# Two six-tile groups of the down projection by seven half-size products, with smaller edits in the delta rule and at both ends of the span

## The chip, the core and the metric

The kernel runs on one core of a Trainium2 chip. The metric is the device time in microseconds of one execution, from launch to the last store. A profile of one execution is at hand as well; its span is the time from the first to the last instruction on the core's engines.

## What is computed

One decoder layer on 1024 tokens of width 1024, in float32 (the leading depth axis has length 1):

```python
def hybrid_layer(x, p_i, ...):
    h = rmsnorm(x, g_mix)
    proj = h @ w_in
    ...
    y_fox = forgetting_attention(fq, fk, fv, fox_f, b_fox_f, fox_q_gain, fox_k_gain)
    ...
    y_sc = sb * causal_dwconv(sc * sv, sc_conv_w)
    ...
    o_dn = gated_delta_rule(l2norm(dq), l2norm(dk_), dv_, g, beta).astype(x.dtype)
    ...
    merged = jnp.sum(jnp.einsum('bsnc,ncd->bsnd', ys, w_branch) * gates, axis=2)
    x = x + merged @ w_o
    u = causal_dwconv(rmsnorm(x, g_ffn) @ w_up, ffn_conv_w)
    u_gate, u_val = jnp.split(u, 2, axis=-1)
    x = x + (jax.nn.silu(u_gate) * u_val) @ w_down
    x = x + jax.nn.sigmoid(rmsnorm(x, g_ple) @ w_ple_gate) * (p_i.astype(x.dtype) @ w_ple)
    return x
```

The inner width of the channel mixer is 2816, that is 22 tiles of 128; `w_down` is 2816 by 1024.

## The kernel before

Activations lie transposed, 128 channels on the partitions and 1024 tokens along the free axis, so a tile is 128 by 1024 and has two halves of 512 tokens (`NB`). Each float32 operand of a large product is split into a high part (rounded to the TensorE's fp32r) and a low part: `split` (lines 128 to 130) copies the high part on ScalarE and subtracts it on VectorE (or GpSimd). `step` (151) then makes three matmuls of 128 by 512: high by high, high by low, low by high. `dense` (159) does this for every k tile and hands the two PSUM banks to an evacuation function. Weights come in by `wraw` into a tile `wr` (two buffers of 1024 columns) and are split by `wsplit` into `wo` (five buffers, high in columns 0 to 511 and low in 512 to 1023).

The program goes: first norm and input projection with attention (`first_norm`, `fox_proj`, `softmax`, `weigh`), the delta rule (`dn_solve`, `dn_prep`, `dn_state`, `dn_out`), with projection tiles used as filler work between, the merge and `W_o`, the up projection, the down projection ("do"), and a last stage that normalises the result, multiplies it by `w_ple_gate` and adds the gated per-layer embedding.

The code is written in program order, and a scheduler at build time sets the order in which each engine's queue gets its instructions. At run time each queue is strictly in order: an instruction that waits holds up what stands behind it on its engine. This is so for SyncE's queue too, which issues nearly all DMAs.

In the up projection, 20 of 22 tiles are made with Strassen's scheme (Winograd's form): `stationary` makes four sums of quarter blocks of the weights and gives seven stationaries, `moving_sums` does the same for the activations, and `seven` (203) runs seven products per pair of output tiles where plain blocking takes eight. It uses three PSUM banks a, b, c per pair: product 1 into a (copied out by ScalarE as s1), 6 added into a (copied out as u2), 7 into b, 5 added into a (copied out as v), then, among the next pair's products, 3 added into a and 4 added into b. The outputs are c + s1, a, b + u2 and b + v. A product that is added into a bank must wait for the copy that was taken from it. There are six banks `mm` and two `sm` in this part.

Down is plain. The 22 activation tiles are taken in `GROUPS` of 2, 4, 4, 4, 4, 4. Tiles 2 and 3 were kept in SBUF; the others come back from DRAM into `wq` (three buffers) and are split by `act`. For each group and each of the four pairs of output tiles (`d2`), one `wload` brings 256 columns of weights per activation tile, `dense` multiplies, and VectorE adds the PSUM bank into `x2` (lines 1172 to 1182), which began as the residual.

The last stage (1184 to 1201): for each of the eight `x2` tiles, `sumsq` squares on ScalarE and adds the squares on GpSimd into two accumulators, and `norm_operand` makes the operands for the gate product. `make_rstd` (283) splits each accumulator, sums over partitions with two matmuls per half into a bank `sm`, and makes the reciprocal root with Ln, Exp and Square on ScalarE and two operations on VectorE. The gate products do not need that factor, but their evacuation does: `ev_f` multiplies the bank by `rs3`, takes the sigmoid, multiplies by the embedding, adds `x2` and stores.

Lines of the delta rule that the change touches: in `add64` (759), two groups of four 128 by 128 float32 matmuls, into `px` and `pt_`, and a VectorE subtraction of the whole `pt_`; in `dn_prep` (803 to 807), the sums of squares of q by four float32 matmuls with one moving column. Line 1271 in the profile is the program's prologue.

## Time and profile before

| | |
|---|---|
| median of three runs | 1966.72 us (1966.46 to 1970.54) |
| profiled execution | 1967.07 us, of which the span is 1965.1 us |
| TensorE matmul busy | 98% of the span |
| VectorE, ScalarE, GpSimd busy | 68%, 46%, 27% |
| DMA, mean over the span | 112 GB/s |
| up projection, down, last stage | from about 1200, 1635 and 1875 us |

The page has the busy time of each engine, the chain of work that ended last, and groups of instructions with the mean of one and the idle time before them. Other views give windows (the busy time of each engine in a stretch of time), waits (who waited for whom), and a timeline (instructions in order of time: start in us from the span's start, duration or the extent of a merged group, engine, line, operation, and in brackets the idle time before it and what ended it). In every view, the mean of one matmul is from its issue until its modelled end, so it is longer than the distance between two that follow each other. A float32 matmul appears as two entries.

### The profile page before, as it was taken

How to read it: one execution, taken by the hardware profiler on the slowest of the kernel's cores; microseconds unless marked ns; L12 is line 12 of the kernel's file. 1: busy time of each engine (PE TensorE's matmuls, PEld its weight loads, DVE VectorE, ACT ScalarE, POOL GpSimd, SP SyncE). 2: the span in 40 equal slices, each digit the busy share in tenths (PEclk: the TensorE clock that was granted, in tenths of full speed). 3: DMA queues.
4: the chain of work that ended last, by engine and by line, in shares of the span. 5: the costliest groups of instructions: out<-in, count | busy, mean ns of one | idle time of the engine just before them, and what ended most of it. 6: DMA issues, size and time to landing. Idle time of an engine off the chain costs nothing.

```text
span 1965.1 us, 25454 instructions
## 1 busy us (share of the span) xinstructions
PE 1930.3 (98%) x9281; PEld 1605.9 (82%) x9281; DVE 1331.0 (68%) x2161; ACT 910.8 (46%) x1651; POOL 531.9 (27%) x431
## 2 busy tenths in 40 slices
PE   8999999999999999999999999999999999999998
PEld 6888888888888888888788787788888887888887
DVE  6878788879388213437766538888888888444564
ACT  6576777677422223433433326555445453211351
POOL 1446343434412221100034112244333330000200
PEclk9999999999999999999999999999999999999999
DMA  4221112221432144347863523212212218322132
GB/s 179 71 91 68 58 60 73 68 69 58 134 127 102 51 148 124 113 175 265 282 223 117 188 107 110 73 61 79 97 64 97 80 49 289 97 86 86 44 119 85
DMA packets 102636, 219.40 MB, mean 112 GB/s; under 512 B 9360, under 2 KB 40432, under 8 KB 102512
## 3 DMA queue, kind: packets, MB, share of 16 engines
q1 hardware_dynamic: 102512, 217.79, 32.8%
q8 instruction: 73, 1.20, 0.3%
q14 instruction: 51, 0.42, 0.1%
HBM read 158.98 MB, written 58.77 MB: 111 GB/s over the span
## 4 chain that ended last, share of the span: by engine, by line
PE 75%; DVE 11%; DMA 5%; ACT 4%; issue 3%; POOL 1%; SPq 0%; DVEq 0%; ACTq 0%; POOLq 0%
PE mm L126 65%; PE sm L126 5%; DVE o L491 1%; DMA sg<-r 1%; PE py L126 1%; PE ev L126 1%; PE pq L637 1%; DVE wo L130 1%; DMA kc<-kdr 1%; DMA y<-yr 1%; DVE o L1094 1%; PE po L126 1%; DMA yr<-r 1%; DVE pl L130 1%; ACT pp L600 1%
## 5 line engine op out<-in xcount | busy, mean ns | idle before, releaser
L126 PE MATMUL mm<-xg,wo 128*128 128x512 f32 x6128 | 1478.9, 392 | 9.4 <-DVE wo L130 2.1
L126 PEld LDWEIGHTS mm<-xg,wo 128*128 128x128 f32 x6128 | 1139.2, 188 | 247.5 <-ACT wo L129 3.5
L126 PE MATMUL mm<-a,wo 128*128 128x512 f32 x1216 | 303.5, 389 | 1.6 <-DVE sg L1029 1.4
L129 ACT ACTIVATE wo<-wr 128x512 fp32r<-128x512 f32 x252 | 157.2, 626 | 278.0 <-PE mm L126 269.9
L126 PEld LDWEIGHTS mm<-a,wo 128*128 128x128 f32 x1216 | 228.2, 188 | 49.8 <-DVE sg L1029 1.8
L130 POOL TENSOR_TENSOR wo<-wr,wo 128x512 fp32r<-128x512 f32 x108 | 150.2, 1393 | 312.4 <-ACT wo L129 299.0
L1181 DVE TENSOR_TENSOR a<-mm,a 128x512 f32<-128x512 f32 x96 | 65.2, 688 | 92.2 <-PE mm L126 92.0
L130 DVE TENSOR_TENSOR wo<-wr,wo 128x512 fp32r<-128x512 f32 x144 | 106.6, 742 | 27.9 <-ACT wo L129 27.4
L280 POOL TENSOR_TENSOR tmp<-tmp,tmp 128x512 f32<-128x512 f32 x21 | 28.1, 1339 | 293.3 <-ACT tmp L278 293.3
L1030 POOL TENSOR_TENSOR a<-a,sg 128x512 f32<-128x512 f32 x28 | 42.4, 1521 | 190.9 <-DVE sg L1029 190.8
L1094 DVE SCALAR_TENSOR_TENSOR o<-cw,cols,o 128x1024 f32<-128x1024 f32 x44 | 77.2, 1755 | 0.0
L491 DVE SCALAR_TENSOR_TENSOR o<-cv,cols,o 128x512 f32<-128x512 f32 x72 | 69.9, 971 | 10.1 <-ACT o L489 9.1
L503 ACT ACTIVATE o<-mm 128x512 f32<-128x512 f32 x60 | 35.7, 595 | 88.3 <-PE mm L126 52.1
L1126 POOL TENSOR_TENSOR cg<-o,cg 128x1024 f32<-128x1024 f32 x22 | 54.8, 2492 | 62.8 <-ACT cg L1125 62.8
L600 ACT ACTIVATE pp<-pp,small 128x512 f32<-128x512 f32 (+2 forms) x96 | 58.4, 610 | 28.9 <-DVE small L594 28.6
L130 DVE TENSOR_TENSOR wo<-wq,wo 128x512 fp32r<-128x512 f32 x48 | 65.4, 1365 | 5.0 <-ACT wo L129 4.2
L129 ACT ACTIVATE wo<-ws 128x512 fp32r<-128x512 f32 x80 | 50.2, 630 | 33.4 <-PE mm L126 33.3
L199 POOL TENSOR_TENSOR ws<-wq,wr 128x512 f32<-128x512 f32 x20 | 44.0, 2199 | 78.9 <-DVE wo L130 73.9
L1094 DVE SCALAR_TENSOR_TENSOR o<-cg,cols,o 128x1024 f32<-128x1024 f32 x44 | 58.4, 1327 | 5.0 <-ACT o L1092 4.9
L130 DVE TENSOR_TENSOR pl<-pq,ph 128x512 fp32r<-128x512 f32 (+1 forms) x80 | 49.9, 629 | 13.9 <-ACT ph L129 13.5
L199 POOL TENSOR_TENSOR ws<-wr 128x512 f32<-128x512 f32 x20 | 35.9, 1797 | 72.3 <-DVE ws L199 46.3
L637 PE MATMUL pq<-cst,pp 128*128 128x128 f32 x288 | 47.0, 273 | 2.0 <-DVE pl L130 1.1
(291 smaller groups left out, 2362.3 us busy)
## 6 DMA issues: line engine op xcount, KB each, us to landing
wr<-win SPq DMA_DIRECT2D x64, 512.0 KB, 3.6
r<-o SPq DMA_DIRECT2D x64, 256.0 KB, 2.5
wq<-wup SPq DMA_DIRECT2D x24, 512.0 KB, 3.5
wr<-wup SPq DMA_DIRECT2D x20, 512.0 KB, 3.7
ad<-o SPq DMA_DIRECT2D x20, 512.0 KB, 3.9
wq<-ad SPq DMA_DIRECT2D x20, 512.0 KB, 4.6
wr<-wdn SPq DMA_DIRECT2D x20, 512.0 KB, 3.7
yr<-r SPq DMA_DIRECT2D x16, 512.0 KB, 5.0
```

The source lines that it names most:

```text
L126: pe[0] = nc.tensor.matmul(o, lhsT=l, rhs=r, start=start, stop=stop, skip_group_check=more)
L129: S.activation(h, x, AF.Copy)
L130: (eng or V).tensor_tensor(out=l, in0=x, in1=h.bitcast(F32), op=ALU.subtract)
L199: (G if e == "g" else V).tensor_tensor(out=o, in0=x, in1=y, op=op)
L491: V.scalar_tensor_tensor(out=o, in0=cv[:, i : i + 512], scalar=col(c0 + i), in1=o, op0=ALU.mult, op1=ALU.add)
L503: S.activation(o, ps, AF.Copy)
L600: S.activation(t[:, :w], t[:, :w], AF.Exp, bias=mn[:, k - 1 : k], scale=-1.0, accum_out=sm[:, i : i + 1])
L637: nc.tensor.transpose(pq[:, c : c + P], pr[s][kt // 4][:, kt % 4 * P : kt % 4 * P + P], ident)
L1030: (V if b == 2 and dt > 5 else G).tensor_tensor(out=m, in0=m, in1=t, op=ALU.add)
L1094: V.scalar_tensor_tensor(out=o, in0=cv[:, i : i + T], scalar=col(c0 + i), in1=o, op0=ALU.mult, op1=ALU.add)
L1126: G.tensor_tensor(out=sg, in0=o, in1=sg, op=ALU.mult)
L1181: V.tensor_tensor(out=x2[dt][:, NB[nb]], in0=ps, in1=x2[dt][:, NB[nb]], op=ALU.add)
```

## The change

1. The groups of down are now of 2, 4, 6, 4 and 6 tiles. A group of six goes to the new function `down`: three pairs of activation tiles are the two halves of k, `moving_sums` makes their sums on VectorE, 21 operand tiles are made (seven in new `bx` buffers, eight in `a`, six in `xg`), and `seven` runs over the four pairs of output tiles, with weights of 768 columns for each half of k, both in `wr`.
2. `seven` now hands every finished bank to a function `ev`. In up it does what was done before. In down, a bank without partner is added into `x2` by VectorE, one with a partner is added to it by VectorE, and the sum goes to `x2` on GpSimd or VectorE.
3. `add64` makes only the 64 by 64 part of `pt_` that is used later. `dn_prep` splits the squares of q and sums them with two fp32r matmuls of two columns per head.
4. At the start, the loads of `cols` and `wsr` are issued by ScalarE's queue, and the first activation tile is loaded in two halves. At the end, the last output half-tile is made and stored in two pieces of 256 columns.
5. The last stage has a scope of its own ("ple"), so its temporaries take the memory of the down stage's when that is done with.

```diff
-GROUPS = [KEPT, (0, 1, 4, 5), (6, 7, 8, 9), (10, 11, 12, 13), (14, 15, 16, 17), (18, 19, 20, 21)]
+GROUPS = [KEPT, (0, 1, 4, 5), (6, 8, 10, 7, 9, 11), (12, 13, 14, 15), (16, 18, 20, 17, 19, 21)]
...
-    Q.dma_start(cols, I["cols"])
+    S.dma_start(cols, I["cols"])
...
-                S.activation(o12, oa, AF.Copy)
+                oev(0, 1, oa)
...
-                V.tensor_tensor(out=c11, in0=c, in1=s1, op=ALU.add)
+                ev(0, 0, c, s1)
...
-        Q.dma_start(wsr, I["wsm"])
+        S.dma_start(wsr, I["wsm"])
...
-            Q.dma_start(xr[kt], I["xT"][kt])
+            for nb in NB if kt == 0 else (slice(0, T),):
+                Q.dma_start(xr[kt][:, nb], I["xT"][kt][:, nb])
...
-                mm(pt_[:, hs(h)], ws[c][:, hs(h)], Tc[c][:, h, :], True, True)
+                mm(pt_[0:64, h * 64 : h * 64 + 64], ws[c][0:64, h * P : h * P + 64], Tc[c][0:64, h, 0:64], True, True)
...
+        qh, ql = pt("qh", 2, 512, F32R), pt("ql", 2, 512, F32R)
         S.activation(qe, qc, AF.Square)
+        split(qh, ql, qe)
         pq_ = evb()
         for h in range(4):
-            mm(pq_[:, h : h + 1], qe[:, hs(h)], Uf[:, 127:128], True, True)
+            mm(pq_[:, 2 * h : 2 * h + 2], qh[:, hs(h)], ones_r[:, 0:2], True, False)
+            mm(pq_[:, 2 * h : 2 * h + 2], ql[:, hs(h)], ones_r[:, 0:2], False, True)
...
-        with phase("do", tmp=8, sg=4):
+        x2 = [ahead[dt] for dt in range(8)]
+        with phase("do", u=4, ws=3):
...
+            def down(f, c0):
+                xs = {k: [] for k in range(1, 8)}
+                room = [xgt] * 6 + [lambda: big(F32R)] * 8 + [lambda: pt("bx", 7, T, F32R)] * 7
...
+                for i in range(3):
+                    b1, b2 = (fetch(k) and acts[k] for k in (f[i], f[i + 3]))
+                    for k, x in ((1, b1[:, NB[0]]), (2, b2[:, NB[0]]), (3, b2[:, NB[1]])):
+                        xs[k].append(operand(x, new))
+                    for k, t in moving_sums(b1, b2, new, "vvvv").items():
+                        xs[k].append(t)
+                def pair(d2):
+                    w = [wraw(I["wdn"][:, c : c + 768], 768) for c in range(c0 + 1536 * d2, c0 + 1536 * d2 + 1536, 768)]
+                    def ev(m, nb, ps, more=None):
+                        o = x2[2 * d2 + m][:, NB[nb]]
+                        V.tensor_tensor(out=o if more is None else more, in0=ps, in1=o if more is None else more, op=ALU.add)
+                        if more is not None:
+                            (G if m == nb else V).tensor_tensor(out=o, in0=o, in1=more, op=ALU.add)
+                    return stationary(*w, 384), ev, lambda: None
+                seven([lambda d2=d2: pair(d2) for d2 in range(4)], xs)
...
+        with phase("ple", tmp=8, sg=4):
             acc = [tmp() for _ in range(2)]
...
+                    gs, n = tmp(), 256 if (dt, nb) == (7, 1) else 512
+                    for c in range(0, 512, n):
```

On TensorE, this is what stands around the sums of squares of the last norm (`sm` is the bank of a sum, `tmp` a part of the squares, `mm` the bank of a gate product). Before:

```order
L126 MATMUL mm_16079<-xg_15991,wo_16043 128x512
L126 MATMUL mm_16079<-xg_16003,wo_16043 128x512
L126 MATMUL mm_16079<-xg_16004,wo_16043 128x512 [waits DVE_49]
L126 MATMUL sm_16028<-tmp_16015,ones_r 128x512 [waits DVE_49]
L126 MATMUL mm_16079<-xg_16003,wo_16043 128x512
L126 MATMUL mm_16120<-xg_15919,wo_16114 128x512
L126 MATMUL mm_16120<-xg_15920,wo_16114 128x512
```

And now:

```order
L126 MATMUL sm_16335<-tmp_16328,ones_r 128x512 [waits DVE_49]
L126 MATMUL mm_16544<-xg_16320,wo_16508 128x512
L126 MATMUL sm_16345<-tmp_16331,ones_r 128x512 [waits Activation_49]
L126 MATMUL sm_16345<-tmp_16332,ones_r 128x512 [waits DVE_49]
L126 MATMUL mm_16585<-xg_16236,wo_16579 128x512 [waits DVE_49]
L126 MATMUL mm_16585<-xg_16237,wo_16579 128x512
```

Before, the sums stood among the first two gate products (banks 16046 and 16079), and the third began behind them without a wait. Now six gate products (16363, 16396, 16437, 16470, 16511, 16544) stand ahead of the sums, and the seventh, 16585, begins with a wait for VectorE: the instruction that its semaphore value belongs to is the evacuation of bank 16363.

On VectorE, behind the same sums (L260 and L264 are the last two operations of each half of the norm factor `rs`, L1196 and L1240 the first of an evacuation). Before:

```order
L260 SCALAR_TENSOR_TENSOR tmp_16022<-tmp_16022,sm_16018 128x512 [waits Activation_49]
L264 SCALAR_TENSOR_TENSOR rs_16009<-tmp_16022,tmp_16021 128x512 [waits DVE_49]
L130 TENSOR_TENSOR wo_16262<-wr_16260,wo_16262 128x512 [waits DMAHW0_49,Activation_49]
L1196 TENSOR_TENSOR tmp_16073<-mm_16046,rs_16009 128x512 [waits DVE_49]
L260 SCALAR_TENSOR_TENSOR tmp_16032<-tmp_16032,sm_16028 128x512 [waits Activation_49]
L264 SCALAR_TENSOR_TENSOR rs_16009<-tmp_16032,tmp_16031 128x512 [waits DVE_49]
```

And now:

```order
L260 SCALAR_TENSOR_TENSOR tmp_16339<-tmp_16339,sm_16335 128x512 [waits Activation_49]
L264 SCALAR_TENSOR_TENSOR rs_16326<-tmp_16339,tmp_16338 128x512 [waits DVE_49]
L260 SCALAR_TENSOR_TENSOR tmp_16349<-tmp_16349,sm_16345 128x512 [waits Activation_49]
L1240 TENSOR_TENSOR tmp_16390<-mm_16363,rs_16326 128x512 [waits DVE_49]
L264 SCALAR_TENSOR_TENSOR rs_16326<-tmp_16349,tmp_16348 128x512 [waits DVE_49]
L1240 TENSOR_TENSOR tmp_16423<-mm_16396,rs_16326 128x512 [waits DVE_49]
```

The evacuation of the first bank stood ahead of the second half's L260, and now stands behind it.

On ScalarE, in the first pair of the first group of six (14968 is bank a of the pair, `u` the copies of it, `wo` the high parts of stationaries, made from the raw weights `wr` or their sums `ws`). Before, ScalarE had only splits like these here, of weights and of activation tiles (`xg` from `wq`):

```order
L129 ACTIVATE wo_15101<-wr_15099 128x512 [waits DMAHW0_49,DVE_49,PE_49]
L129 ACTIVATE wo_15104<-wr_15099 128x512 [waits DVE_49,PE_49]
L129 ACTIVATE wo_15165<-wr_15163 128x512 [waits DMAHW1_49,DVE_49,PE_49]
L129 ACTIVATE wo_15168<-wr_15163 128x512 [waits DVE_49,PE_49]
L129 ACTIVATE xg_15357<-wq_15355 128x1024 [waits DMAHW5_49,PE_49]
```

And now:

```order
L129 ACTIVATE wo_15085<-wr_15041 128x384 [waits PE_49,Activation_49]
L227 ACTIVATE u_14972<-mm_14968 128x512 [waits PE_49]
L129 ACTIVATE wo_15099<-wr_14958 128x384 [waits DMAHW0_49]
L129 ACTIVATE wo_15113<-ws_15046 128x384 [waits DVE_49,PE_49,Activation_49]
L230 ACTIVATE u_14973<-mm_14968 128x512 [waits PE_49]
L213 ACTIVATE u_15056<-mm_15053 128x512
```

L227 is the copy u2 after product 6, and L230 the copy v after product 5 of the first pair, for which its product 3 waits. Between them now stand the high parts of the first pair's fourth stationary (15099) and of the second pair's sixth (15113), which is made from `ws_15046`, a sum that takes in the second pair's second half of weights (`wr_15043`). SyncE issues the load of `wr_15043` when the subtraction that ends the use of `wr_14958` (the low part of 15099, on VectorE) is done, since `wr` has two buffers. On TensorE the first group of six stands in this order: products 1, 2, 7 and 6 of the first pair, 1 and 2 of the second, 5 and 3 of the first, 6 of the second, and so on. The second group of six has the same order at its start.

More of the change, by code (lines that the diff above doesn't have):

```diff
@@ L208, in seven @@
             if new:
-                w, (c11, c12, c21, c22), done = new()
+                w, ev, done = new()
                 a, b, c = mmb(), mmb(), mmb()
@@ L214, in seven @@
             if old:
-                oa, ob, ou2, ow, o12, o21, odone = old
+                oa, ob, ou2, ow, oev, odone = old
                 product(oa, ow[3](), xs[3], True)
-                S.activation(o12, oa, AF.Copy)
+                oev(0, 1, oa)
             if new:
                 product(c, w[2](), xs[2])
-                V.tensor_tensor(out=c11, in0=c, in1=s1, op=ALU.add)
+                ev(0, 0, c, s1)
             if old:
                 product(ob, ow[4](), xs[4], True)
-                V.tensor_tensor(out=o21, in0=ob, in1=ou2, op=ALU.add)
+                oev(1, 0, ob, ou2)
                 odone()
@@ L230, in seven @@
                 S.activation(v, a, AF.Copy)
-                V.tensor_tensor(out=c22, in0=b, in1=v, op=ALU.add)
-                old = a, b, u2, w, c12, c21, done
+                ev(1, 1, b, v)
+                old = a, b, u2, w, ev, done
     def plain(ws, xs, outs):
@@ L763, in add64 @@
             for h in range(4):
-                mm(pt_[:, hs(h)], ws[c][:, hs(h)], Tc[c][:, h, :], True, True)
+                mm(pt_[0:64, h * 64 : h * 64 + 64], ws[c][0:64, h * P : h * P + 64], Tc[c][0:64, h, 0:64], True, True)
             V.tensor_tensor(out=Xs[c], in0=Xs[c], in1=px, op=ALU.subtract)
-            V.tensor_tensor(out=Tc[c], in0=Tc[c], in1=chunk(pt_), op=ALU.subtract)
+            t = Tc[c][0:64, :, 0:64]
+            V.tensor_tensor(out=t, in0=t, in1=pt_[0:64, 0:256].rearrange("p (h i) -> p h i", i=64), op=ALU.subtract)
         def to128(c):
@@ L1136, in up @@
                 w = stationary(wpair(I["wup"][f])[0], wraw(I["wup"][NF + f]), 512)
-                cg, cv = padded()
-                return w, spans(cg, cv), lambda: gated(f, cg, cv)
+                cs = padded()
+                def ev(m, nb, ps, more=None):
+                    o = cs[m][:, 2 + 512 * nb : 514 + 512 * nb]
+                    if more is None:
+                        S.activation(o, ps, AF.Copy)
+                    else:
+                        V.tensor_tensor(out=o, in0=ps, in1=more, op=ALU.add)
+                return w, ev, lambda: gated(f, *cs)
             halves = {(h, nb): [] for h in range(2) for nb in range(2)}
@@ L1168, in act, with new, ev @@
                 acts[f] = h, l
-            x2 = [ahead[dt] for dt in range(8)]
+            def down(f, c0):
+                xs = {k: [] for k in range(1, 8)}
+                room = [xgt] * 6 + [lambda: big(F32R)] * 8 + [lambda: pt("bx", 7, T, F32R)] * 7
+                def new():
+                    return room.pop()()
+                for i in range(3):
[6 more added lines that the diff above has]
+                    w = [wraw(I["wdn"][:, c : c + 768], 768) for c in range(c0 + 1536 * d2, c0 + 1536 * d2 + 1536, 768)]
+                    def ev(m, nb, ps, more=None):
+                        o = x2[2 * d2 + m][:, NB[nb]]
[4 more added lines that the diff above has]
+                seven([lambda d2=d2: pair(d2) for d2 in range(4)], xs)
             c0 = 0
             for g in GROUPS:
+                n = len(g)
+                if n == 6:
+                    down(g, c0)
+                    c0 += 6144
+                    continue
                 for f in g:
                     act(f)
-                n = len(g)
                 for d2 in range(4):
@@ L1194, in ev_f @@
                         Q.dma_start(part, pdr[dt][:, NB[nb]])
-                    g = tmp()
-                    V.tensor_tensor(out=g, in0=ps, in1=rs3[:, NB[nb]], op=ALU.mult)
-                    S.activation(g, g, AF.Sigmoid)
-                    V.tensor_tensor(out=g, in0=part, in1=g, op=ALU.mult)
-                    V.tensor_tensor(out=g, in0=g, in1=x2[dt][:, NB[nb]], op=ALU.add)
-                    Q.dma_start(out[dt][:, NB[nb]], g)
+                    gs, n = tmp(), 256 if (dt, nb) == (7, 1) else 512
+                    for c in range(0, 512, n):
+                        g, s = gs[:, c : c + n], slice(512 * nb + c, 512 * nb + c + n)
+                        V.tensor_tensor(out=g, in0=ps[:, c : c + n], in1=rs3[:, s], op=ALU.mult)
+                        S.activation(g, g, AF.Sigmoid)
+                        V.tensor_tensor(out=g, in0=part[:, c : c + n], in1=g, op=ALU.mult)
+                        V.tensor_tensor(out=g, in0=g, in1=x2[dt][:, s], op=ALU.add)
+                        Q.dma_start(out[dt][:, s], g)
                 dense(wload(I["wpg"][dt]), KT, xg3, ev_f)
```

2 lines of the change are left out of this document (1 added, 1 removed).

## The prediction

> **What bounds the kernel now.** First the busy times of the page: microseconds, share of the span, instructions.
>
> ```profile
> PE 1930.3 (98%) x9281; PEld 1605.9 (82%) x9281; DVE 1331.0 (68%) x2161; ACT 910.8 (46%) x1651; POOL 531.9 (27%) x431
> ```
>
> TensorE works in all but 34.8 us of the span. A matmul that goes is therefore gained in full, and so is lost each microsecond in which TensorE is made to wait. Second, the windows by stage (bounds and length, then busy time and instructions of PE, PEld, DVE, ACT, POOL, the granted clock, DMA share, GB/s): delta rule, up, down, last stage, and the very end.
>
> ```profile
> 720.00:860.00 140.00, 138.87 (x853) 122.86 (x852) 49.78 (x144) 52.88 (x142) 25.61 (x20) 1.00 0.36 114
> ...
> 1250.00:1630.00 380.00, 377.54 (x1663) 311.61 (x1662) 316.05 (x318) 185.24 (x277) 145.65 (x115) 1.00 0.22 77
> ...
> 1700.00:1880.00 180.00, 180.00 (x796) 149.04 (x795) 93.82 (x125) 50.21 (x76) 18.72 (x14) 1.00 0.25 77
> 1880.00:1966.00 86.00, 79.26 (x350) 65.22 (x348) 41.84 (x62) 26.26 (x37) 0.00 (x0) 0.99 0.33 110
> ...
> 1955.00:1966.00 11.00, 4.26 (x19) 3.19 (x17) 3.46 (x5) 0.84 (x2) 0.00 (x0) 0.92 0.13 48
> ```
>
> Plain down has no gap at all: 180.00 of 180.00. Strassen's scheme in up, with VectorE busy 316 us of 380 where down has 94 of 180, loses 2.46 us in 380, some 20 pairs of tiles. In the last stage TensorE rests only after its last matmul.
>
> The sum is made against the profiled execution, 1967.07 us, of which 2.0 lie outside its span of 1965.1; the median of the runs, 1966.72, is 0.35 below it.
>
> **Down: 72 matmuls go.** The order of instructions has 5696 matmuls `mm<-xg` for 6128, 1408 `mm<-a` for 1216, and 168 `mm<-bx`: 72 fewer in all. Per group of six and pair, seven products of nine matmuls against eight, four pairs, two groups, 2 x 4 x 9 = 72 again. A stretch of down gives the distance of two matmuls; a later row, from the last stage, is the cover of the next part.
>
> ```profile
> 1651.63 48.67 PE L126 MATMUL mm<-xg,wo 128*128 128x512 f32 x214
> ...
> 1882.69 17.64 PE L126 MATMUL mm<-xg,wo 128*128 128x512 f32 x77
> ```
>
> (48.67 - 0.39) / 213 = 0.2267 us, the 0.39 being the last one's own length; 72 x 0.2267 = **-16.3 us**. That work isn't hidden anywhere, so it counts in full.
>
> **The norm sums of the last stage.** By the order, six gate products now stand ahead of the second half's sums, one per `mm` bank, and the seventh waits for VectorE's evacuation of the first. That evacuation stands behind the second half's L260, which needs ScalarE's Square. Before, only two products were ahead. The timeline of that place (start, length, the wait before it in brackets):
>
> ```profile
> 1880.35 0.40 PE L126 MATMUL sm<-tmp,ones_r 128*128 128x512 f32 x1
> ```
>
> ```profile
> 1880.83 1.28 ACT L257 ACT_TABLE_LOAD   x1 [1.93 <-PE sm L126]
> ```
>
> ```profile
> 1888.41 0.68 DVE L1196 TENSOR_TENSOR tmp<-mm,rs 128x512 f32<-128x512 f32 x1
> ...
> 1890.40 0.69 DVE L260 SCALAR_TENSOR_TENSOR tmp<-tmp,sm 128x512 f32<-128x512 f32 x1 [1.31 <-ACT tmp L259]
> 1891.13 0.69 DVE L264 SCALAR_TENSOR_TENSOR rs<-tmp,tmp 128x512 f32<-128x512 f32 x1
> ```
>
> From the first half's sum ScalarE and VectorE need 1890.40 - 1880.35 = 10.05 us until the second half's L260. Before, this was covered: four more banks of 24 matmuls, 4 x 24 x 0.2267 = 21.8 us (the 77 matmuls without a wait above), while the first evacuation came at 1888.41. Now nothing is left to do. On the old clock: L260 at 1890.40, the evacuation in L264's old place at 1891.13, 0.69 long, 0.05 of handover: 1891.87. TensorE would have issued the seventh product four matmuls after the first sum, at 1880.35 + 0.91 = 1881.26. So it rests 10.6 us: **+10.6**. Behind the wait on TensorE stands the rest of the program, so no other work fills it.
>
> **The clock after that rest.** The start of the program is the only place where TensorE works after a long rest; it had rested 6.3 us.
>
> ```profile
> 6.30 2.10 PE L126 MATMUL sm<-xg,wsp 128*32 128x512 f32 x4 [6.30 <-ACT xg L270]
> 8.47 3.61 PE L126 MATMUL mm<-xg,wo 128*128 128x512 f32 x8
> ...
> 13.31 1.08 PE L126 MATMUL mm<-xg,wo 128*128 128x512 f32 x4
> ```
>
> Eight matmuls there stand (3.61 - 0.40) / 7 = 0.46 us apart, and 0.23 at 13.31. Eight at 0.23 more than normal are **+1.8**; 0 if the clock stays, and 3.5 if the slow stretch is all from 6.30 to 13.31. The window 1955 to 1966 above has a granted clock of 0.92, while the last stage as a whole has 0.99: the clock goes down some microseconds after the last matmul. The Trainium skill, "TensorE: Matmul & The Clock Gate", section "Part 1: The HAM clock gate (the "warmup" mystery)", says that the clock falls to half after about 3.4 us without work, and needs about as much sustained work to come back. By that rule this wait would cost an estimated 1.7 us more, and the sum would come out the same; the trace agrees with the halving at the start (0.46 against 0.23), and no row of before shows it after a gap in mid-program.
>
> **Waits within the groups of six.** In the first pair of each group, product 3 waits for the copy v. By the order, v stands on ScalarE behind a stationary made from a sum that takes in the next pair's second half of weights, whose load goes out only when the first pair's last low part is subtracted. The rows (the line groups and the DMA issues):
>
> ```profile
> L230 ACT ACTIVATE u<-mm 128x512 f32<-128x512 f32 x20 | 12.0, 598 | 79.9 <-PE mm L126 79.9
> ...
> L130 DVE TENSOR_TENSOR wo<-ws,wo 128x512 fp32r<-128x512 f32 x60 | 40.9, 685 | 6.9 <-ACT wo L129 6.8
> ...
> L199 POOL TENSOR_TENSOR ws<-wr 128x512 f32<-128x512 f32 x18 | 24.2, 1343 | 55.7 <-DVE ws L199 46.3 <-DMA wr<-wup 6.5 <-ACT wo L129 2.9
> ```
>
> ```profile
> wr<-wdn SPq DMA_DIRECT2D x20, 512.0 KB, 3.7
> ...
> wr<-wdn SPq DMA_DIRECT2D x4, 256.0 KB, 2.7
> ```
>
> Operations on 384 columns are taken at three quarters. After product 6: copy u2 0.60, high part 0.45, subtraction 0.51, a load of 384 KB 3.2 (between the two), GpSimd's sum 1.0, VectorE's sum 0.51, high part 0.45, v 0.60, and about 0.3 for the handovers: 7.6 us. TensorE has three products of nine matmuls meanwhile, 6.1 us. So it waits 1.5, twice: **+3.0** (0 to 6 with the load between 2.7 and 3.7 and VectorE free or not). The other six pairs have their loads a pair earlier; for all eight I take up's own rate, 2.46 / 20 = 0.12 each: **+1.0**.
>
> **Delta rule.** Solve and preparation, where the page shows a float32 matmul as two entries:
>
> ```profile
> 686.10 1.14 PE L126 MATMUL sm<-w,TT 64*64 64x64 f32 x16
> 687.17 19.80 PE L126 MATMUL mm<-xg,wo 128*128 128x512 f32 x86
> ...
> 718.18 0.95 PE L126 MATMUL ev<-cst,qe 128*128 128x1 f32 x8
> 718.99 1.14 PE L126 MATMUL sm<-bv,X 128*128 128x128 f32 x8
> ...
> 722.95 1.05 PE L126 MATMUL ev<-qc,ks 128*128 128x128 f32 x8
> 723.76 0.48 PE L126 MATMUL mm<-xg,wo 128*128 128x512 f32 x1
> ```
>
> The 64 entries into `pt_` go from the form of 722.95 (0.81 / 8 = 0.101) to that of 686.10 (1.07 / 16 = 0.067): 64 x 0.034 = **-2.2**; filler stands around them, so it counts. The sums of q stay 64 entries. Float32 by one column is 0.101 (718.18); fp32r by two columns isn't shown. It lies between the 0.067 of a small block, -2.2, and 0.115 if loading the weights limits it, +0.9; I take **0**, the row that is nearest in weights loaded. The eight new splits on ScalarE and VectorE are hidden by filler: those engines are busy 53 and 50 of the 140 us there. Without that cover they would cost 8 x 1.3 = 10 us.
>
> **Start and tail.**
>
> ```profile
> 0.73 1.28 ACT L109 ACT_TABLE_LOAD   x1 [0.73 <-PEq L1271]
> ...
> 5.53 1.33 ACT L270 ACTIVATE xg<-xr,cols 128x512 fp32r<-128x512 f32 x2 [2.18 <-DMA xr<-xT]
> ```
>
> The first operand waits for `xr`, which was third in SyncE's queue and is now first, about 0.9 earlier, in two halves. But `cols` and `wsr` now go out from ScalarE's queue, behind the table load that ends at 2.01. Half of it I count: **-0.4** (-1.0 to +0.8).
>
> ```profile
> 1959.30 0.69 DVE L1196 TENSOR_TENSOR tmp<-mm,rs 128x512 f32<-128x512 f32 x1 [2.63 <-PE mm L126]
> ...
> 1961.41 0.69 DVE L1199 TENSOR_TENSOR tmp<-tmp,a 128x512 f32<-128x512 f32 x1
> ```
>
> ```profile
> outT<-tmp SPq DMA_DIRECT2D x16, 256.0 KB, 2.9
> y<-yt SPq DMA_DIRECT2D x32, 64.0 KB, 1.9
> ```
>
> The last evacuation is a chain of 2.8 us and a store. In two pieces, each operation at about 0.42 and the two interleaved, it ends after some 2.5, and its last store is half as large, half-way from 2.9 to 1.9: 0.3 + 0.5 = **-0.8** (-1.3 to 0).
>
> **Sum.** -16.3 - 2.2 - 0.4 - 0.8 = -19.7; +10.6 + 1.8 + 3.0 + 1.0 = +16.4. Together -3.3: 1967.1 - 3.3 = **1963.8 us**, 0.15% below the median. About 0.2% is what a measurement of this kernel can tell from no change.
>
> **Rivals.**
>
> *The wait for the norm is short.* If the factor's chain is made earlier, by ScalarE standing ahead of where it stood, the 12.4 us of wait and clock fall away: 1967.1 - 19.7 + 4 = 1951.4; with 2 us left of it 1953. For it speaks that the before trace has no such wait; against it, that the order ties the first evacuation to the second L260, with the four table loads between. Chance 0.10.
>
> *The clock stays.* Then 1962.0. For it speaks that the start is the first work of all, so that nothing shows a return to work in mid-program; against it the 0.46 there and the 0.92 at the end. Chance 0.17.
>
> *The squares come late: slower.* Fourteen additions on GpSimd (L280) stand between the last `x2` and the sums.
>
> ```profile
> L280 POOL TENSOR_TENSOR tmp<-tmp,tmp x14: 1282/1292/1742, 1837.4 to 1874.5; 128x512 f32<-128x512 f32 x14
> ```
>
> ```profile
> L199 POOL TENSOR_TENSOR ws<-wq,wr 128x512 f32<-128x512 f32 x19 | 42.7, 2247 | 78.9 <-DVE wo L130 73.9 <-issue 5.0
> ```
>
> All of `x2` is now complete only after product 4 of the last pair of a group of six. By the order, TensorE has 118 matmuls between that pair's last product and the first sum, 26.8 us. The additions begin some 4.8 us into it, by the copies, VectorE's additions and the square ahead of them, and take 14 x 1.34 = 18.8, and 0.6 for a copy: 24.2. It fits as long as one takes under 1.53. At 2.25, which GpSimd's additions beside VectorE's work in up need, the sums are 10 us late: 1974. For it: VectorE adds to `x2` at the same time; against it: 1292 ns median in down before. Chance 0.12, at 1966 to 1974, half of it beyond 1970.6.
>
> *Two buffers of weights starve every pair: slower.* Each pair's weights take both `wr` buffers, where before one group of columns was one buffer and the other was ahead. If the six later pairs wait 2 us each as well, 1963.8 + 12 = 1976. It decides where the 14.3 us of a pair's 63 matmuls don't cover load, sums and splits; the load, two sums at 1.34, a copy and a subtraction come to some 8, so 0.07.
>
> That the change doesn't do what it says is excluded by the 72 matmuls fewer in the order.
>
> **How the numbers follow.** Forecast 0.54, its own range 1960.5 to 1968 from the bounds of the clock, the waits and the start. With the rival of the clock (0.17, mostly the same range) and half of the late squares it holds 0.8 from 1958.5 to 1970. Faster by over 0.2% (below 1962.8): the short wait, most of the clock's rival, and a fifth of the forecast, 0.10 + 0.13 + 0.12 = 0.35. Slower (above 1970.6): 0.06 + 0.07 + 0.01 = 0.14. Within: 0.51.
>
> **What would show it.** TensorE idle by 10 us in front of one product of the last stage, released by VectorE's L1240, right: the norm; distances near 0.46 behind it: the clock. Two waits of 1 to 2 us for ScalarE's L230 in down, 72 fewer matmuls of 0.227, entries of 0.067 in the solve. It would be wrong if the sums wait for GpSimd, if all pairs of six show waits, or if no wait stands in the last stage.

## The result, and the profile after

The changed kernel takes 1976.71 us (median of four runs, 1975.72 to 1977.87), beside 1967.51 for the kernel before on the same chip: 1.0044 times as long, 95% interval 1.0031 to 1.0057. So it is slower by 9.2 us; the forecast was 3 us faster, and the range ended at 1970. The profiled execution has a span of 1976.1 us where before had 1965.1, 11.0 us more.

The busy times of the changed kernel, from the page:

```profile
PE 1923.4 (97%) x9209; PEld 1594.5 (81%) x9209; DVE 1386.7 (70%) x2258; ACT 948.2 (48%) x1746; POOL 584.7 (30%) x471
```

72 fewer matmul entries, as forecast, and TensorE idle for 52.7 us instead of 34.8. But its busy time fell by only 6.9 us, not by the 16.3 of 72 matmuls, although some small ones were made cheaper besides. A matmul's busy time is longer while the granted clock is low (in the rows below 0.79 us where 0.39 is usual), so two things have to be looked at: idle time, and the clock. The windows of down and of the last stage, with PEclk after the POOL column:

```profile
1700.00:1880.00 180.00, 170.89 (x731) 138.24 (x730) 120.47 (x177) 67.28 (x129) 48.34 (x39) 0.98 0.24 71
1880.00:1977.00 97.00, 80.78 (x344) 65.94 (x342) 47.26 (x68) 34.85 (x54) 19.17 (x14) 0.93 0.30 101
```

Down, which had no idle time in this stretch, now has 9.1 us, and the clock is below 1.00 in both rows. The waits of TensorE (engine and line that waited, engine, tile and line that released it: total, times, longest) say for what:

```profile
PE mm L126 <- DVE tmp L1240: 10.1, 1, 10.1
...
PE mm L126 <- ACT wo L129: 5.7, 4, 2.9
PE mm L126 <- ACT u L230: 5.0, 3, 2.5
PE sm L126 <- DMA kc<-kdr: 2.9, 2, 2.6
```

The first is the forecast wait for the evacuation in the last stage, predicted at 10.6. The next two are mainly the groups of six: in the timeline five waits over 0.6 us stand there, of 2.54, 0.77, 0.62, 2.23 and 2.89, together 9.05 us, where the forecast had 4.0 for all of them. The three long ones:

```profile
1714.13 1.52 PE L126 MATMUL mm<-bx,wo 128*128 128x512 f32 x3 [2.54 <-ACT u L230]
...
1821.60 0.96 PE L126 MATMUL mm<-bx,wo 128*128 128x512 f32 x3 [2.23 <-ACT u L230]
...
1847.38 1.64 PE L126 MATMUL mm<-bx,wo 128*128 128x512 f32 x3 [2.89 <-ACT wo L129]
```

The granted clock falls after the first and the third of these. Five windows of the changed kernel, two in the delta rule, two in down and the one behind the norm's wait:

```profile
546.94:550.35 3.41, 3.41 (x19) 3.41 (x18) 0.00 (x0) 0.00 (x0) 0.00 (x0) 0.50 0.57 157
...
850.73:854.14 3.41, 3.41 (x9) 2.63 (x9) 0.00 (x0) 0.38 (x1) 0.00 (x0) 0.50 0.00 0
1714.30:1717.71 3.41, 3.41 (x9) 2.65 (x10) 3.38 (x4) 1.09 (x3) 2.83 (x3) 0.50 0.00 0
1847.42:1850.83 3.41, 3.41 (x8) 2.73 (x9) 3.21 (x6) 2.85 (x6) 0.00 (x0) 0.50 0.01 2
...
1913.69:1919.10 5.41, 5.41 (x13) 4.25 (x14) 5.38 (x10) 3.66 (x6) 0.00 (x0) 0.50 0.18 51
```

In each TensorE is busy throughout at a clock of 0.50; in down it makes 8 or 9 matmuls where 15 fit (3.41 / 0.2267). A window of 3.41 us at half clock thus costs about 1.7 us: four of them 6.8, and the 5.41 us behind the norm's wait 2.7. The profiled execution before has no such window in its stages. So this profile has lost 9.5 us to the clock that the other has not; 3.4 of them were lost in two places of the delta rule, where the groups of six play no part.

The chain at the norm in the changed kernel, on TensorE and VectorE:

```profile
1902.92 0.62 PE L126 MATMUL sm<-tmp,ones_r 128*128 128x512 f32 x2
1913.69 0.79 PE L126 MATMUL mm<-xg,wo 128*128 128x512 f32 x1 [10.15 <-DVE tmp L1240]
```

```profile
1912.34 0.69 DVE L260 SCALAR_TENSOR_TENSOR tmp<-tmp,sm 128x512 f32<-128x512 f32 x1 [1.19 <-ACT tmp L259]
1912.95 0.68 DVE L1240 TENSOR_TENSOR tmp<-mm,rs 128x512 f32<-128x512 f32 x1
```

L1240, the evacuation of the first bank, follows the second L260, and TensorE goes on when it ends.

### The profile page after: what moved, and what is told of

Read it like the earlier page. It is cut to its first block, busy times and chain, and to the rows that moved or that the text cites. A ratio compares the mean times of both kernels' runs of the same rounds, so it can differ in the third digit from the quotient of the medians.

```text
span 1976.1 us, 25567 instructions
## 1 busy us (share of the span) xinstructions
PE 1923.4 (97%) x9209; PEld 1594.5 (81%) x9209; DVE 1386.7 (70%) x2258; ACT 948.2 (48%) x1746; POOL 584.7 (30%) x471
## 4 chain that ended last, share of the span: by engine, by line
PE 72%; DVE 12%; ACT 5%; DMA 5%; issue 4%; POOL 2%; SPq 0%; DVEq 0%; ACTq 0%; POOLq 0%
PE mm L126 62%; PE sm L126 5%; DVE o L492 1%; DVE wo L130 1%; PE py L126 1%; PE ev L126 1%; PE pq L638 1%; DMA yr<-r 1%; DMA sg<-r 1%; DMA kc<-kdr 1%; POOL ws L199 1%; PE po L126 1%; DMA y<-yr 1%; DVE yr L965 1%; ACT wo L129 1%
## 5 line engine op out<-in xcount | busy, mean ns | idle before, releaser
L126 PE MATMUL mm<-xg,wo 128*128 128x512 f32 x5696 | 1393.4, 394 | 18.1 <-DVE tmp L1240 10.1
L126 PEld LDWEIGHTS mm<-xg,wo 128*128 128x128 f32 x5696 | 1061.2, 189 | 242.0 <-DVE tmp L1240 10.6
L126 PE MATMUL mm<-a,wo 128*128 128x512 f32 x1408 | 357.8, 391 | 1.5 <-DVE sg L1034 1.4
L126 PEld LDWEIGHTS mm<-a,wo 128*128 128x128 f32 x1408 | 265.6, 189 | 57.7 <-DVE sg L1034 1.8
L129 ACT ACTIVATE wo<-wr 128x512 fp32r<-128x512 f32 (+1 forms) x252 | 154.1, 615 | 184.9 <-PE mm L126 159.2
L130 DVE TENSOR_TENSOR wo<-wr,wo 128x512 fp32r<-128x512 f32 (+1 forms) x144 | 105.9, 739 | 53.0 <-ACT wo L129 52.3
L129 ACT ACTIVATE wo<-ws 128x512 fp32r<-128x512 f32 (+1 forms) x112 | 65.9, 598 | 84.3 <-PE mm L126 49.7
L199 POOL TENSOR_TENSOR ws<-wr 128x512 f32<-128x512 f32 (+1 forms) x28 | 45.1, 1609 | 159.6 <-DMA wr<-wdn 87.7
L199 POOL TENSOR_TENSOR ws<-wq,wr 128x512 f32<-128x512 f32 x20 | 44.0, 2199 | 79.5 <-DVE wo L130 74.5
L130 DVE TENSOR_TENSOR wo<-ws,wo 128x512 fp32r<-128x512 f32 (+1 forms) x84 | 59.5, 713 | 9.0 <-ACT wo L129 8.8
L126 PE MATMUL mm<-bx,wo 128*128 128x512 f32 x168 | 49.4, 403 | 9.1 <-ACT u L230 4.8
L230 ACT ACTIVATE u<-mm 128x512 f32<-128x512 f32 x28 | 16.7, 595 | 86.5 <-PE mm L126 86.5
```

The source lines that it names most:

```text
L126: pe[0] = nc.tensor.matmul(o, lhsT=l, rhs=r, start=start, stop=stop, skip_group_check=more)
L129: S.activation(h, x, AF.Copy)
L130: (eng or V).tensor_tensor(out=l, in0=x, in1=h.bitcast(F32), op=ALU.subtract)
L199: (G if e == "g" else V).tensor_tensor(out=o, in0=x, in1=y, op=op)
```

## The experiments

**Is the norm's wait the price of six products ahead of the sums?** The last two groups of down change places, so that a plain one is last:

```diff
-GROUPS = [..., (6, 8, 10, 7, 9, 11), (12, 13, 14, 15), (16, 18, 20, 17, 19, 21)]
+GROUPS = [..., (6, 8, 10, 7, 9, 11), (12, 14, 16, 13, 15, 17), (18, 19, 20, 21)]
```

> The changed kernel with the last two groups of down in the other order: six tiles (12, 14, 16, 13, 15, 17), then a plain group of four (18 to 21). The number of matmuls stays. By the order only two gate products then stand ahead of the norm sums, as before the change. If the wait of 10.15 us in front of the seventh gate product, with the slow clock after it, is the price of six products standing ahead of the sums, it goes whole: about 10.3 + 2.6 = 12.9 us less than the changed kernel, near 1964 us, and no TensorE wait over 1 us in the last stage. Rival: GpSimd's additions of squares are what is late; then a wait of the sums for GpSimd or ScalarE of some microseconds stays, and the gain is under 6 us.

Measured: 1977.19 us, 1.0050 (1.0034 to 1.0067): no gain at all. The norm's wait did go: no wait of TensorE for that evacuation is left. In its place waits stand where the second group of six begins, right behind the first (its timeline, TensorE):

```profile
1762.24 0.50 PE L126 MATMUL mm<-bx,wo 128*128 128x512 f32 x1 [2.54 <-ACT wo L129]
...
1767.47 1.22 PE L126 MATMUL mm<-a,wo 128*128 128x512 f32 x2 [1.70 <-DVE a L130]
1771.71 3.39 PE L126 MATMUL mm<-a,wo 128*128 128x512 f32 x6 [3.02 <-ACT a L129]
```

```profile
1764.29:1777.94 13.65, 7.96 (x16) 4.07 (x15) 13.21 (x22) 6.54 (x13) 0.31 (x1) 0.50 0.46 143
```

The first of these waits is for weights; the others, and one of 0.58 us between them, are for `a` and `bx`: the operands of the second group, which have the first group's buffers and can't be made ahead. VectorE is busy 13.21 of 13.65 us, and the clock is low through four windows. So it is the plain group between the two groups of six that hides the making of operands; the runs with the groups apart, below, bear this out. Neither of the two expectations had this, and the edit only traded one wait for the other.

**What are the edits beside the half-size products worth?** `GROUPS` as before the change, all else as changed.

```diff
-GROUPS = [KEPT, (0, 1, 4, 5), (6, 8, 10, 7, 9, 11), (12, 13, 14, 15), (16, 18, 20, 17, 19, 21)]
+GROUPS = [KEPT, (0, 1, 4, 5), (6, 7, 8, 9), (10, 11, 12, 13), (14, 15, 16, 17), (18, 19, 20, 21)]
```

> The changed kernel with the old groups of 2, 4, 4, 4, 4, 4 tiles: no half-size products in down, the edits of the delta rule, of the start, of the tail and the scope of the last stage stay. By the sum of the prediction these edits are worth 2.2 + 0.4 + 0.8 = 3.4 us: 1964 us. Rival: the trace of the changed kernel stood 2 us behind the one of before at the end of up, because of two stretches of 3.4 us at half clock in the delta rule and a longer wait for the load of kc; if these belong to the edits, the result is 1967 us or more, with the same two stretches in its trace; if they fall there by chance, they are in other places or absent.

Measured: 1964.24 us, 0.9986 (0.9976 to 0.9996), 1.9 us less than before in the medians where 3.4 were forecast; the interval allows both. Down by half-size products, with the waits and the clock that it brings, thus costs the changed kernel some 11 us net (1.0044 against 0.9986), though 16.3 us of matmuls go. Its trace has three windows at half clock, at 102, 850 and 1263 us: other places than in the changed kernel's, but for 850.

**Are the waits in the groups of six those of two weight buffers?** A third `wr` buffer, alone or with the plain group last, has no room: the pool `me` would take 42.4 KB per partition where 39.0 are left, so neither variant has a time. Instead the first half of a pair's weights goes to `wq` (three buffers), so that `wr` holds one half of each of two pairs:

```diff
-w = [wraw(I["wdn"][:, c : c + 768], 768) for c in range(c0 + 1536 * d2, c0 + 1536 * d2 + 1536, 768)]
+c = c0 + 1536 * d2
+w = [pt("wq", 3, 1024), wraw(I["wdn"][:, c + 768 : c + 1536], 768)]
+Q.dma_start(w[0][:, :768], I["wdn"][:, c : c + 768])
```

> The changed kernel with the first half of a pair's raw weights in a wq buffer (three of them) instead of wr, so that wr holds one half per pair and both loads go out a pair earlier. Groups as in the changed kernel. If the loads bound to two wr buffers are what TensorE waits for in the groups of six (9 us and two stretches at half clock), these waits all but go: 9 to 12 us less than the changed kernel, 1965 to 1968 us, with the 10 us wait of the last stage still there. Rival: the queue order on ScalarE and VectorE sets the waits; then at most 4 us are gained.

Measured: 1961.45 us, 0.9972 (0.9959 to 0.9985): 15 us less than the changed kernel (0.9972 against 1.0044 is 14) where 9 to 12 were forecast, and faster than before. Two windows of down, first of the changed kernel, then of this one:

```profile
1640.00:1780.00 140.00, 136.01 (x588) 110.59 (x587) 114.24 (x169) 55.55 (x98) 28.42 (x21) 0.99 0.43 139
1780.00:1870.00 90.00, 84.88 (x364) 68.97 (x363) 59.99 (x89) 33.50 (x63) 25.10 (x20) 0.98 0.16 46
```

```profile
1640.00:1780.00 140.00, 138.65 (x612) 114.38 (x611) 120.43 (x180) 60.27 (x106) 32.21 (x23) 1.00 0.43 134
1780.00:1870.00 90.00, 90.00 (x399) 74.55 (x398) 54.37 (x80) 40.45 (x73) 30.17 (x24) 1.00 0.19 59
```

In the second window all 5.1 us of idle time are gone, in the first all but one wait of 1.35, and the clock is 1.00. The norm's wait stands unchanged:

```profile
1896.09 4.21 PE L126 MATMUL mm<-xg,wo 128*128 128x512 f32 x9 [10.14 <-DVE tmp L1242]
```

So the two waits are separate, and ScalarE's queue order, with which the prediction explained the waits in part, is not enough to make them: here too L230 (at 1707.22) stands behind two high parts of weight sums (1703.14 and 1705.23), but the loads come earlier, and TensorE does not wait for it.

**Plain group last, groups of six apart.** Once with two buffers and once with the first half in `wq`:

```diff
+GROUPS = [KEPT, (0, 1), (4, 6, 8, 5, 7, 9), (10, 11, 12, 13), (14, 16, 18, 15, 17, 19), (20, 21)]
```

> The changed kernel with groups of 2, 2, 6, 4, 6, 2 tiles: the last group plain as in the run with the plain group last, but the two groups of six kept apart by a plain one. Two gate products stand ahead of the norm sums. If the run with the plain group last lost its 13 us because the second group of six had no plain group ahead, in whose time its operands are made, then this one shows neither that nor the norm wait: the waits of the first and third kind stay (about 9 us and 3 of clock), so 1977 - 13 = about 1964 us. Rival: the norm factor's wait and the new waits are one shortage (VectorE late with all of x2 work), which only moves; then about 1975 us again.

> Both: groups of 2, 2, 6, 4, 6, 2 and the first half of the weights in wq. If the three causes are separate (six gate products ahead of the sums, groups of six side by side, two raw buffers), this gives the whole gain of the 72 matmuls: 1964.2 of the kernel without groups of six, less 16.3, plus 1 to 3 us of small waits, 1949 to 1952 us. Rival: some of the waits inside a group remain because of ScalarE's queue: 1953 to 1958.

Measured: 1973.8 us, 1.0037 (1.0024 to 1.0051), and 1963.83, 0.9991 (0.9979 to 1.0002). Both miss the forecast. The norm's wait is away in both, and the second group of six, with a plain group of four ahead, has no wait for operands in either. But in the last stage short waits for the norm's operands (L271) come in, 2.9 and 2.4 us together, and the first group of six now comes 43 us after up and is not ready: with two buffers TensorE waits there for an operand `a` (3.53 us in one piece), with `wq` for weights. TensorE and ScalarE in the second of the two:

```profile
1676.75 3.51 PE L126 MATMUL mm<-bx,wo 128*128 128x512 f32 x7 [7.35 <-ACT wo L129]
```

```profile
1673.94 1.15 ACT L129 ACTIVATE xg<-wq 128x512 fp32r<-128x512 f32 x2 [2.35 <-DMA wq<-ad]
1676.18 0.94 ACT L129 ACTIVATE wo<-wq 128x384 fp32r<-128x384 f32 x2 [1.08 <-DMA wq<-wdn]
```

The last activation tile comes out of `wq` at 1673.94, and only then the weights for which TensorE waits. That fits with a `wq` buffer, lent to the weights, being missing for activation tiles; no run separates this from the short time behind up, which makes the first of the two runs wait as well.

A third order, with `wq`:

```diff
+GROUPS = [KEPT, (0, 1, 4, 5), (6, 8, 10, 7, 9, 11), (12, 13), (14, 16, 18, 15, 17, 19), (20, 21)]
```

> Groups of 2, 4, 6, 2, 6, 2 tiles, the first half of the weights in wq. In the run with groups of 2, 2, 6, 4, 6, 2 one wait of 7.35 us with 6.8 us at half clock stood at the first group of six, which came 43 us after the end of up; here it comes 65 us after, as in the changed kernel, where only 1.35 us were left there with wq. The second group of six has a plain group of two ahead (22 us), not of four. If a group of six needs some 40 us of plain work ahead for its operands, the wait moves to the second group and the result is 1960 to 1964 us again; if 22 us are enough, 1950 to 1953 us.

Measured: 1960.02 us, 0.9952 (0.9936 to 0.9967). The wait at the first group is 1.11 us as in the run with `wq` alone; at the second group three of 0.60, 1.56 and 1.06 stand, with 3.41 us at half clock, all for parts of weights. VectorE, which makes the low parts of weights and operands in one queue, is busy 35.6 of the 36 us from 1758 to 1794, so 22 us of plain work ahead are not enough for it. Two more waits, of 0.61 and 1.71 us, stand in the last stage, for the norm's operands (L271) behind the short last group.

**Half of it.** One group of six only, `wq` for its weights:

```diff
+GROUPS = [KEPT, (0, 1, 4, 5), (6, 8, 10, 7, 9, 11), (12, 13, 14, 15), (16, 17, 18, 19), (20, 21)]
```

> Only one group of six (6 to 11), the first half of its weights in wq, all else plain in groups of 2, 4, 4, 4, 2. 36 matmuls go, not 72. By the same reasons 1964.2 - 8.2 + 0.5 to 1.5 = about 1957 us, with no wait over 1 us in down. Rival as above: 1960 us.

Measured: 1960.88 us, 0.9969 (0.9956 to 0.9982). The one group loses 1.21 us, the last stage 1.40 and 1.25, waiting for its operands behind the short last group; the time is the rival's, but not by the rival's cause.

**The norm's wait by its length.** The changed kernel with `wq`, and the additions of squares of the second half of the tokens on VectorE:

```diff
-                sumsq(acc, x2[dt], dt == 0)
+                sumsq(acc, x2[dt], dt == 0, (G, V))
```

> The changed kernel with the first half of the weights in wq, as in the run of that name (1961.45), and the additions of squares of the second half of the tokens on VectorE instead of GpSimd. GpSimd then adds 7 times, not 14, and by the order 4.6 gate products instead of six stand ahead of the norm sums, so that TensorE has some 35 matmuls (7.9 us) left when the first sum goes out, where it had four (0.9). If the wait is the 11 us of the norm factor's chain less what is left in the six banks, it shrinks from 10.1 to about 3.6 us, and the slow clock behind it from 5.4 us to 3.4 us or nothing: 7 to 9 us less, 1953 to 1955 us. Rival: GpSimd was not what put the sums late, the sums now wait for VectorE instead, and the wait stays at 8 to 10 us: 1960 us.

Measured: 1954.86 us, 0.9930 (0.9916 to 0.9943). The additions of squares (shortest, median and longest in ns, then the first and the last start), in the changed kernel and here:

```profile
L280 POOL TENSOR_TENSOR tmp<-tmp,tmp x14: 1283/1301/1748, 1879.8 to 1897.9; 128x512 f32<-128x512 f32 x14
```

```profile
L280 POOL TENSOR_TENSOR tmp<-tmp,tmp x7: 1293/1630/1648, 1866.4 to 1876.3; 128x512 f32<-128x512 f32 x7
L280 DVE TENSOR_TENSOR tmp<-tmp,tmp x7: 692/1605/1778, 1866.9 to 1878.6; 128x512 f32<-128x512 f32 x7
```

They start within 12 us instead of 18, the sums stand ahead of 1.4 more products, and the wait and its clock shrink:

```profile
1892.53 12.80 PE L126 MATMUL mm<-xg,wo 128*128 128x512 f32 x48 [2.37 <-DVE tmp L1242]
```

```profile
1893.57:1896.98 3.41, 3.41 (x9) 2.64 (x8) 3.41 (x7) 2.72 (x6) 0.00 (x0) 0.50 0.47 154
```

2.37 us where 3.6 were forecast, against the rival's 8 to 10.

The last edit is on top of this one, for this norm alone: both Ln, then both Exp, then both Square, so that two table loads stand in the chain instead of four. The main lines of it:

```diff
-            newton(r[:, NB[nb]], *rsqrt(ps, 1.0 / D))
...
+                sums.append(ps)
...
+            for t, ps in zip(ts, sums):
+                S.activation(t, ps, AF.Ln, scale=1.0 / D)
+            for t, y in zip(ts, ys):
+                S.activation(y, t, AF.Exp, scale=-0.5)
+            for nb, (t, y, ps) in enumerate(zip(ts, ys, sums)):
+                S.activation(t, y, AF.Square)
...
```

> The kernel with the squares split (1954.86 us) and the norm factor of the last stage made in another order on ScalarE: both Ln, then both Exp, then both Square, so that two table loads of 1.28 us stand in the chain instead of four. If the wait that is left (2.37 us, with 3.4 us at half clock behind it) is the chain's length, it shortens by about 2.5 us and the wait is gone, with the slow stretch: 1954.9 - 2.4 - 1.7 = about 1951 us. Rival: the first half's factor comes later now, since its Exp stands behind the second Ln, and the wait stays.

Measured: 1949.41 us, 0.9918 (0.9899 to 0.9938), the fastest, 17 us below the kernel before. The wait that is left:

```profile
1884.90 5.30 PE L126 MATMUL mm<-xg,wo 128*128 128x512 f32 x22 [0.67 <-DVE tmp L1256]
```

No window at half clock follows it.

**The delta rule by parts.** The kernel before with one of the change's edits each: in `add64` alone, and in `dn_prep` alone.

```diff
-                mm(pt_[:, hs(h)], ws[c][:, hs(h)], Tc[c][:, h, :], True, True)
+                mm(pt_[0:64, h * 64 : h * 64 + 64], ws[c][0:64, h * P : h * P + 64], Tc[c][0:64, h, 0:64], True, True)
...
```

```diff
...
-            mm(pq_[:, h : h + 1], qe[:, hs(h)], Uf[:, 127:128], True, True)
+            mm(pq_[:, 2 * h : 2 * h + 2], qh[:, hs(h)], ones_r[:, 0:2], True, False)
+            mm(pq_[:, 2 * h : 2 * h + 2], ql[:, hs(h)], ones_r[:, 0:2], False, True)
...
```

> The kernel before with one edit, the 64 by 64 part of pt_ in add64. By the prediction 64 entries go from 0.101 to 0.067 us: 2.2 us faster, -0.11%. If the gain is lost on the way, because the filler that stood there is only moved, it is nothing.

> The kernel before with one edit, the sums of squares of q by fp32r matmuls of two columns. By the prediction no difference (between -2.2 and +0.9 us). Rival: the stretch of 3.4 us at half clock at about 850 us, which the traces of the changed kernel and of most runs with this edit show and the one of before does not, belongs to the edit; then it stands in this trace too, and the kernel is 1.5 to 2 us slower. If it is there by chance, it is absent or elsewhere.

Measured: 1965.99 us, 0.9990 (0.9981 to 0.9999), 2.0 less, for the solve, as forecast; and 1969.96, 1.0010 (0.9999 to 1.0021), for the sums of q, which leaves open whether they cost nothing or up to 4 us. On the window at 850 us these two traces say more. First the solve alone, which does not have the edit of q, then the sums of q:

```profile
848.33:851.74 3.41, 3.41 (x13) 3.12 (x14) 1.11 (x5) 1.23 (x2) 1.27 (x1) 0.50 0.00 0
```

```profile
848.33:851.74 3.41, 3.25 (x22) 3.02 (x23) 2.18 (x9) 0.80 (x2) 0.00 (x0) 1.00 0.00 0
1260.68:1264.10 3.42, 3.42 (x10) 2.63 (x9) 0.67 (x2) 0.00 (x0) 0.00 (x0) 0.50 0.42 153
```

The half clock at 850 us is there without the edit of q and absent with it, so it does not belong to that edit.

**A second profile of the changed kernel.**

> The changed kernel once more, for a second profile. If the waits of the groups of six and of the norm are fixed by the order, they are there with the same lengths to 0.5 us, and about 1976.7 us. If the stretches at half clock at 547 and 851 us come from how the gaps there happen to lie against a fixed grid of windows, and not from the edits, they are not both there in this profile, or others are.

Measured: 1977.09 us, 1.0048 (1.0033 to 1.0063). The norm's wait is 10.15 us again. The waits over 0.6 us in the groups of six are 2.23, 2.06, 2.34 and 1.44, together 8.07 for 9.05: the same places but for one, and two of them (2.06 for 0.77, 1.44 for 2.89) differ by more than the 0.5 us expected. The stretches at 547 and 851 us are both there again (at 545.3 and 849.1), so this run alone does not decide on them. But in down the stretches at half clock moved:

```profile
1712.67:1716.08 3.41, 2.35 (x10) 1.97 (x11) 2.85 (x4) 2.32 (x5) 1.59 (x2) 1.00 0.01 2
...
1739.98:1743.39 3.41, 3.41 (x10) 2.67 (x9) 2.07 (x4) 1.26 (x3) 0.00 (x0) 0.50 0.40 114
1821.90:1825.31 3.41, 3.41 (x9) 2.68 (x9) 3.38 (x4) 1.23 (x3) 3.41 (x3) 0.50 0.00 0
```

## Why the prediction was wrong

What held, term by term:

- **72 matmuls**: 9209 entries for 9281, each still 0.2267 apart at full clock.
- **The norm's wait**: 10.15 us for 10.6, at the place and for the reason that was given; two runs shortened it by the two means that the reason names, products in hand and the chain's length.
- **The solve**: 2.0 us for 2.2, in a run of its own.
- **The start**: TensorE is 0.4 us ahead at the eleventh microsecond (11.52 for 11.92), as forecast, but by luck: its first matmul comes later (6.77 for 6.30), the eight of 8.47 start together with those of 8.48, and it is these eight that take 3.20 us for 3.61. An earlier return of the clock explains that: its record in the trace begins, at 1.00, at 11.05 us for 11.75, and in the eleven profiles with this edit anywhere from 9.84 to 12.84.
- **The tail**: from the last bank's first evacuation to the end of the span it was 5.8 us (1959.30 to 1965.1) and is 5.1 (1970.96 to 1976.1), 0.7 for 0.8.

What failed:

- **The waits within the groups of six** were taken at 4.0 us. They are 9.05 in idle time, 9.1 with the small ones. The chain in the first pair was right in its links and short in its sum, 1.5 us of wait for 2.5 and 2.2: GpSimd's first sum starts 3.43 us after the load's issue, where 3.2 was counted, and VectorE's sum takes 1.33 us beside GpSimd's second one, where 0.51 was counted. SyncE, GpSimd and VectorE there:

```profile
1707.14 0.33 SPq L136 DMA_DIRECT2D wr<-wdn  x1
```

```profile
1710.57 1.02 POOL L199 TENSOR_TENSOR ws<-wr 128x384 f32<-128x384 f32 x1 [6.76 <-DMA wr<-wdn]
```

```profile
1711.62 1.33 DVE L199 TENSOR_TENSOR ws<-ws,wr 128x384 f32<-128x384 f32 x1 [4.51 <-POOL ws L199]
```

  More weighs that "the other six pairs have their loads a pair earlier" was wrong. The longest wait, 2.89 us at 1847.38, is for a later pair's weights. SyncE, VectorE and ScalarE there:

```profile
1833.82 10.10 SPq L136 DMA_DIRECT2D wr<-wdn  x2
```

```profile
1840.11 2.13 DVE L130 TENSOR_TENSOR wo<-ws,wo 128x384 fp32r<-128x384 f32 x2
1842.16 0.68 DVE L1202 TENSOR_TENSOR a<-mm,a 128x512 f32<-128x512 f32 x1
1842.76 0.77 DVE L199 TENSOR_TENSOR ws<-wr,ws 128x384 f32<-128x384 f32 x1
```

```profile
1846.80 0.52 ACT L129 ACTIVATE wo<-wr 128x384 fp32r<-128x384 f32 x1 [3.20 <-DMA wr<-wdn]
```

  The second of SyncE's two loads goes out near 1843.6, when the sum L199 has read the `wr` buffer. That sum stands in VectorE's queue behind two subtractions for stationaries and an addition of a bank into `x2`, 2.7 us of work, and so the weights come at 1846.8. That was the rival of the two buffers, given 7 in 100 because one pair's matmuls seemed to cover load and sums. The pricing counted the work of a load, not the queue in which the buffer's last reader stands. The run with `wq` shows that it is the two buffers: with earlier loads one wait of 1.35 us is left of these 9.05. The rival's 1976 us agrees with the result by luck: its sizes were others, six waits of 2 us and no clock for them.
- **The clock** was counted once, behind the ten microseconds of the norm (1.8; it is 2.7). That waits of 2 to 3 us also bring half clock was not thought of: 3.4 us in down. The Trainium skill, "TensorE: Matmul & The Clock Gate", section "Part 1: The HAM clock gate (the "warmup" mystery)", has the clock fall after an idle window of some 3.4 us; here a wait of 2.54 us was enough, so the measurement decides. What the Trainium skill says there of the window, that it is free-running, agrees with the distances of 89, 342, 381 and 399 times 3.413 us in the last section.
- **The delta rule** was taken at -2.2, and the solve gave that. But the profile of the changed kernel has lost 3.4 us there by two windows at half clock, and TensorE waits 2.6 us for a load of kc, where the longest was 1.7 before. The sums of q stand 0.114 us apart for 0.101, which is 0.8 us more; 0.9 was the upper bound. The two windows are not a price of the edits as far as the traces show. The rest at 848 us is 1.12 or 1.13 us long in all fourteen profiles, the one of before included; in ten of them it lies within one window, and half clock follows nine times; in the other four, before among them, a border of two windows cuts it, and the clock stays at 1.00. The wait for kc varies from 0.65 to 2.69 us. So the profile before escaped what its kernel meets in other executions. Beside the experiments 68 were taken; in 31 the mean granted clock is 0.998 or lower, which is at least 5.9 us at half clock, and the stretch behind the last matmul has at most 3.1 of that in the fourteen profiles. The profiled one has 1.000.

So the forecast's -3.3 becomes +11 in the profiled execution mainly by 5 us more of waits in the groups of six, 3.4 of clock behind them, 0.9 more of clock at the norm, and almost 5 ahead of up, of which the clock is 3.4: at the start of up the changed kernel is 2.3 us behind the one before (1203.68 for 1201.41 after the same wait of 1.65), where the forecast had it 2.6 ahead.

The rival of late squares did not come about: an addition took 1301 ns and TensorE did not wait for the sums. But the additions begin only at 1879.8, where they began at 1837.4 before, and so it is they that put six products ahead of the sums: begun within 12 us instead of 18 they put fewer there. The first square starts at 1878.07, when the last addition that reads `u`, a buffer of down, has ended (1877.44). That fits with the memory which the last stage takes over from down; no run tests it.

## What to carry to other kernels

Where products are made fewer but each needs more preparation, count for every buffer of the raw input who reads it last and in which queue that reader stands; a second buffer can cover one load's time and still not the reader's turn. A wait of 2 to 3 us on a TensorE that is otherwise busy can cost 1.7 us more in clock, so several middling waits weigh more than the waits view says (here 9.05 us of waits brought 3.4 of clock). And before a wait is moved by another order of the work, see what its present place hides: here a plain group hid the operands of the next one.

## What the runs showed of the hardware

The granted clock is 1.00 or 0.50, and in the changed kernel the changes lie on a grid: the low stretches begin at 546.94, 850.73, 1714.30, 1847.42 and 1908.86 us, and their distances from the first are 89, 342, 381 and 399 times 3.413 us. A wait counts by how it lies in that grid. The wait for L230 at the first group of six is 2.54 us in the first profile, all of it in one window of 3.41 us, and the next window is at half clock. In the second profile it is 2.23 us (1711.50 to 1713.73), a border at 1712.67 cuts it in two, and the clock stays at 1.00. The wait of 2.23 us at the second group of six in the first profile is cut too, at 1820.11, and costs no clock. Where exactly the threshold lies was not tried, but in the run with the plain group last two windows of down stand on either side of it: in the one from 1706.26 TensorE rests 1.77 us (busy 1.64 of 3.41), and the clock stays; in the one from 1760.87 it rests 1.95 (busy 1.47 of 3.42), and the next window is at half clock. Among small matmuls less rest is enough, the 1.13 us at 848 us. Executions of one kernel spread over 4 to 8 us (1962.17 to 1969.96 for the kernel before, in one set of 13), and such windows have a share in it: one window of 3.413 us lowers the mean granted clock of an execution by 0.0009, and in the set of the kernel before beside the run with `wq` the 15 executions at 0.999 took 1965.7 us in the mean, the 8 at 0.998 took 1966.6, and the 3 below that 1970.6. One more thing: VectorE and GpSimd slow each other where both add. In the run with the squares split, VectorE's additions take 1605 ns in the median where the shortest takes 692, and GpSimd's 1630 where the median is 1301 in the changed kernel, in which the additions are GpSimd's alone (rows above).
